# A state space layer beside projections: the scan over 512 steps becomes block Toeplitz products and a scan over 64 chunks

## The chip, the cores and the metric

The kernel runs on one core of a Trainium2 chip, in one launch. The metric is the device time of one execution in microseconds (us). The engines named below are TensorE (PE; its weight loads are PEld), VectorE (DVE), ScalarE (ACT), GpSimd (POOL) and SyncE (SP), which here issues nearly all DMAs. Each engine works through its own instructions in order.

## The reference

Three transformer-like blocks on 512 tokens of width 1024, in float32. The change lies in the first block, in its mixer: an attention and a state space branch are computed from the same projection and merged by gates. The state space branch has 16 groups of 16 channels with 64 complex states each:

```python
# per group g and state n: ab = exp((a_re + i a_im) * dt),  bb = (ab - 1) / (a_re + i a_im) * b
bu_re = einsum('bsgc,gnc->bsgn', ug, bb_re);  bu_im = einsum('bsgc,gnc->bsgn', ug, bb_im)
# x[t] = ab * x[t-1] + bu[t], complex, over the 512 tokens
_, _, xr, xi = lax.associative_scan(combine, (a_re_t, a_im_t, bu_re, bu_im), axis=1)
y = einsum('bsgn,gcn->bsgc', xr, c_re) - einsum('bsgn,gcn->bsgc', xi, c_im) + d_skip * ug
y = gelu(y);  return y * sigmoid(y @ w_glu + b_glu)
```

## The kernel before

**Layout.** Tokens lie along the free dimension (512), channels on the 128 partitions. A large product is made of three fp32r matmuls, high part times high part, times low part, and low times high (`mm3`, L105): so each weight tile is loaded, cast to its high part on ScalarE (L304) and given its low part on VectorE or GpSimd (L305). The class `Weights` keeps a fixed list of keys: three raw tiles, four split ones, loads up to three tiles ahead, issued by SP in the order of the list. A projection of one 128-channel tile is 24 matmuls of 512 columns.

**Order.** The order of instructions on every engine is written out by hand: it is the order in which the Python code issues them.

**The opening (`first_half`).** The input is normalised and modulated tile by tile into `xn`; for each of 8 tiles TensorE runs four matmuls for the attention's values (`banks`, L1126) and two for the state input (`us`, L1128), in plain float32. Beside it VectorE reduces the modulation's weights (`wa`), ScalarE modulates (L1078) and casts (L1082), and GpSimd builds, by doubling, the tables of cosines and sines (`Rotations.level`), and scales `b` (`scaled`). The callables of `more` say what is issued in which of the 8 steps.

**The stretch the change rewrites (`ssm_states`).** Eleven projections (`queue`, queries, keys and three gates) are interleaved with the scan. The states are taken two groups at a time, 2 x 64 on the partitions, in 8 rounds. In round i `drive` computes `bu` (six matmuls of 32 rows, copies by ScalarE), `table` doubles the rotation table to 512 steps (ScalarE, GpSimd, VectorE), `turn_back` and `turn_back2` rotate the drive back by the states' angle, `scan` runs two real scans of 512 steps with the decay `mag` (VectorE), `turn_forth` and `turned` rotate forth again, `emit` multiplies with `c` (four passes of float32), and `collect` adds the skip term into `y`, 32 rows at a time. The rotations' products are shared out between VectorE and GpSimd. The rounds are pipelined by one: round n+1 turns back while round n turns forth.

**After it.** `attention` runs 8 heads (scores `z`, softmax on VectorE and ScalarE, transposes, values) interleaved with more gate projections; its first projection still carries round 7's `emit` and `collect`. `gelu` and `glu` use `y` later. Then come the merging products, the first feed-forward part and the two further blocks, which the change does not touch.

Of the kernel before, what the change touches and what calls it, by code (L numbers as in the profile page):

```python
# [13 lines left out]
P = 128  # L14
# [8 lines left out]
_COLS = (("ident", P), ("ones", P), ("mask", P), ("count", 32), ("bada", 48), ("gmix", 8),  # L23
         ("gffn", 8), ("gfin", 8), ("bgate", 16), ("are", 8), ("aim", 8), ("ldt", 8), ("dskip", 2),
# [8 lines left out]
class Core:  # L33
# [4 lines left out]
    def __init__(self, ctx, tc, a):  # L38
# [17 lines left out]
        self.pav = ps("pav", 1)  # L56

# [4 lines left out]
        self.ident, self.ones = self.vec["ident"], self.vec["ones"]  # L62
        eps = self.const.tile([P, 1], F32, name="eps")
# [629 lines left out]

class SsmParams:


    def __init__(self, k, vec):
        self.k = k
        self.t = {n: k.const.tile([P, 8], F32, name=f"s_{n}") for n in (
            "dt", "mag", "ang", "n", "r", "sin", "cos", "half", "nr", "ni", "den", "fr", "fi", "x")}  # L700
        self.lr, self.li, self.ldt = vec["are"], vec["aim"], vec["ldt"]

    def load(self):
        self.b = self.k.tmp("b")
        self.k.nc.sync.dma_start(out=self.b, in_=self.k.a["bssm"])

    def decay(self):
        nc, t = self.k.nc, self.t
        nc.scalar.activation(t["dt"], self.ldt, AF.Exp)
        nc.gpsimd.tensor_tensor(t["mag"], self.lr, t["dt"], ALU.mult)  # L710
        nc.scalar.activation(t["mag"], t["mag"], AF.Exp)

    def angle(self):
# [8 lines left out]
        V.tensor_tensor(ang, self.li, t["dt"], ALU.mult)  # L722
# [41 lines left out]
    def scaled(self):  # L764
        k, t = self.k, self.t
        G = k.nc.gpsimd
        cut = lambda p, h: p[:, h * 256:h * 256 + 256].rearrange("p (i c) -> p i c", i=8)
        bre, bim = cut(self.b, 0), cut(self.b, 1)
        frb = t["fr"][:, :].unsqueeze(2).to_broadcast([P, 8, 32])
        fib = t["fi"][:, :].unsqueeze(2).to_broadcast([P, 8, 32])  # L770
        self.bb = k.tmp("bb")
        tt = k.tmp("bt")
        bbr, bbi, t1, t2 = cut(self.bb, 0), cut(self.bb, 1), cut(tt, 0), cut(tt, 1)
        G.tensor_tensor(bbr, bre, frb, ALU.mult)
        G.tensor_tensor(t1, bim, fib, ALU.mult)
        G.tensor_tensor(bbr, bbr, t1, ALU.subtract)
        G.tensor_tensor(bbi, bim, frb, ALU.mult)
        G.tensor_tensor(t2, bre, fib, ALU.mult)
        G.tensor_tensor(bbi, bbi, t2, ALU.add)

    def transpose(self):
        k = self.k
        ps = k.pz.tile([P, S], F32, tag="z", name=k.uid("bt"))
        for j in range(4):
            cs = slice(j * P, (j + 1) * P)
            k.nc.tensor.transpose(ps[:, cs], self.bb[:, cs], k.ident)
        self.bh, self.bl = k.gt("bth"), k.gt("btl")
        k.split(self.bh, self.bl, ps)


class Rotations:
# [3 lines left out]
    def __init__(self, k, params):  # L795
        self.k = k
        self.c = k.gt("c64", F32)[:, :].rearrange("p (i t) -> p i t", i=8)
        self.s = k.gt("s64", F32)[:, :].rearrange("p (i t) -> p i t", i=8)
        self.p = params.t["cos"], params.t["sin"]
        k.nc.vector.memset(self.c[:, :, 0:1], 1.0)  # L800
        k.nc.vector.memset(self.s[:, :, 0:1], 0.0)
        self.big = []

    def level(self, j):
        k, G = self.k, self.k.nc.gpsimd
        c, s = self.c, self.s
        pc, pn = self.p
        n = 1 << j
        if j < 6:
            lo, up = slice(0, n), slice(n, 2 * n)  # L810
            cb = pc[:, :].unsqueeze(2).to_broadcast([P, 8, n])
            sb = pn[:, :].unsqueeze(2).to_broadcast([P, 8, n])
            x = k.tmp("cx")[:, :].rearrange("p (i t) -> p i t", i=8)
            u, v = x[:, :, 0:n], x[:, :, 32:32 + n]
            G.tensor_tensor(u, c[:, :, lo], cb, ALU.mult)
            G.tensor_tensor(v, s[:, :, lo], sb, ALU.mult)
            G.tensor_tensor(c[:, :, up], u, v, ALU.subtract)
            G.tensor_tensor(u, c[:, :, lo], sb, ALU.mult)
            G.tensor_tensor(v, s[:, :, lo], cb, ALU.mult)
            G.tensor_tensor(s[:, :, up], u, v, ALU.add)  # L820
        else:
            self.big.append((pc, pn))
        if j < 8:
            c2 = k.const.tile([P, 8], F32, name=f"s_pc{j}")
            s2 = k.const.tile([P, 8], F32, name=f"s_ps{j}")
            x2 = k.const.tile([P, 8], F32, name=f"s_px{j}")
            G.tensor_tensor(x2, pn, pn, ALU.mult)
            G.tensor_tensor(c2, pc, pc, ALU.mult)
            G.tensor_tensor(s2, pc, pn, ALU.mult)
            G.tensor_tensor(c2, c2, x2, ALU.subtract)  # L830
            G.tensor_scalar(s2, s2, 2.0, 0.0, ALU.mult, ALU.add)
            self.p = c2, s2


class Ssm:

    def __init__(self, k, vec, params, tables):
        self.k, self.vec, self.params, self.tables = k, vec, params, tables  # L840
        self.u, self.uh, self.ul = [], [], []
        self.y = [k.gt("y", F32) for _ in range(2)]
        self.turn, self.half, self.work, self.bu, self.cw, self.ps = {}, {}, {}, {}, {}, {}
        for half in range(2):
            for ri in range(2):
                w = k.gt("cw", F32)[:, :].rearrange("p (q c) -> p q c", q=4)
                k.nc.sync.dma_start(out=w, in_=k.a["cssm"][half, ri])
                self.cw[half, ri] = w

    def table(self, i, j):  # L850

        if i > 7:
            return
        k, nc = self.k, self.k.nc
        c64, s64, big = self.tables.c, self.tables.s, self.tables.big
        if j == 0:
            c, s = k.tmp("rc"), k.tmp("rs")
            x, y = k.tmp("rx"), k.tmp("ry")
            nc.scalar.copy(c[:, :64], c64[:, i])
            nc.scalar.copy(s[:, :64], s64[:, i])  # L860
            self.turn[i] = c, s
            self.half[i] = x, y
        c, s = self.turn[i]
        x, y = self.half[i]
        n = 64 << j
        cj, sj = (p[:, i:i + 1] for p in big[j])
        lo, up, hi = slice(0, n), slice(n, 2 * n), slice(256, 256 + n)
        nc.scalar.activation(x[:, hi], s[:, lo], AF.Copy, scale=sj)
        nc.scalar.activation(y[:, hi], c[:, lo], AF.Copy, scale=sj)
        if j < 2:  # L870
            nc.scalar.activation(x[:, lo], c[:, lo], AF.Copy, scale=cj)
            nc.scalar.activation(y[:, lo], s[:, lo], AF.Copy, scale=cj)
# [1138 lines left out]
```

## Time and profile before

| | us |
|---|---|
| Median of 3 runs | 2599.25 (2597.18 to 2599.49) |
| The profiled execution | 2599.66 |
| Its span, first to last instruction | 2597.9 |
| TensorE busy | 2513.9 |
| VectorE busy | 1338.1 |
| ScalarE busy | 1021.3 |
| GpSimd busy | 659.3 |

Busy times are from the profile of one execution; its own time is 1.76 us longer than its span. The mean granted clock of TensorE was 0.986 of full speed. Of 40 equal slices of the span (65 us each), TensorE is busy nine tenths or more in all but the first three and the last; the first, with the opening, has 8 tenths, the next two, with the state space stretch, 7 each. The weights make most of the 252 MB that DMAs move, 97 GB/s in the mean.

### The profile page before, as it was taken

Reading aid. Unit: us, or ns where it says so; the run is one execution under the profiler, and the core shown is the slowest. Engines: PE = TensorE matmul, PEld = TensorE weight load, DVE = VectorE, ACT = ScalarE, POOL = GpSimd, SP = SyncE. Lnnn points to the kernel's source line nnn. Section 1 sums busy time; section 2 is a strip of 40 time slices with the busy share of each in tenths; the row PEclk is TensorE's granted clock in tenths of the full one; section 3 lists DMA queues with packets and bytes.
Section 4 is the critical chain, followed back from the end, with each engine's and each line's share of the span. In section 5 each row is a group of like instructions: output and inputs, shape, how many; then the busy total and the mean of one; then the engine's idle time right before and its main releaser. Section 6 shows DMA issues by size and latency. Waiting matters only on the chain.

```text
span 2597.9 us, 30110 instructions
## 1 busy us (share of the span) xinstructions
PE 2513.9 (97%) x11724; PEld 2060.5 (79%) x11724; DVE 1338.1 (52%) x1909; ACT 1021.3 (39%) x1667; POOL 659.3 (25%) x589
## 2 busy tenths in 40 slices
PE   8779999999999999999999999999999999999998
PEld 4557788888888888777888888888888778888887
DVE  6997675543534322885644432634423775633322
ACT  3536535332433322555533322433323655433322
POOL 7773121000311100564411100311102463311101
PEclk9889999999999999999999999999999999999999
DMA  6113453433223232212232333232232212222332
GB/s 261 49 58 113 148 173 122 138 98 98 83 97 97 96 98 92 74 49 82 82 98 98 95 91 99 82 98 97 85 106 79 73 52 95 77 97 96 93 97 69
DMA packets 80498, 252.14 MB, mean 97 GB/s; under 512 B 8930, under 2 KB 12770, under 8 KB 80356
## 3 DMA queue, kind: packets, MB, share of 16 engines
q1 hardware_dynamic: 79780, 249.70, 29.9%
q8 instruction: 92, 1.51, 0.2%
q10 hardware_dynamic: 576, 0.52, 0.1%
q14 instruction: 50, 0.41, 0.0%
HBM read 248.09 MB, written 2.10 MB: 96 GB/s over the span
## 4 chain that ended last, share of the span: by engine, by line
PE 80%; DVE 13%; ACT 3%; POOL 2%; issue 2%; DMA 0%; SPq 0%; DVEq 0%; ACTq 0%; POOLq 0%
PE mm L107 24%; PE mm L109 24%; PE mm L108 24%; PE mm L340 1%; DVE keep L1618 1%; DVE wa L503 1%; PE mm L1126 1%; PE n L368 1%; DVE wl L305 1%; PE z L1597 1%; POOL x L1522 1%; DVE fs L1514 1%; DVE acc L437 1%; DVE x L1522 1%; PE mm L608 1%
## 5 line engine op out<-in xcount | busy, mean ns | idle before, releaser
L305 DVE TENSOR_TENSOR wl<-wr,wh 128x1024 fp32r<-128x1024 f32 (+2 forms) x383 | 455.0, 1193 | 919.4 <-ACT wh L304 919.2
L304 ACT CAST wh<-wr 128x1024 fp32r<-128x1024 f32 (+3 forms) x444 | 430.8, 979 | 547.1 <-PE mm L108 507.9
L107 PE MATMUL mm<-xh,wh 128*128 128x512 f32 x1568 | 617.5, 394 | 0.1
L109 PE MATMUL mm<-xh,wl 128*128 128x512 f32 x1568 | 611.9, 390 | 0.0
L108 PE MATMUL mm<-xl,wh 128*128 128x512 f32 x1568 | 611.7, 390 | 0.0
L109 PEld LDWEIGHTS mm<-xh,wl 128*128 128x128 f32 x1568 | 295.3, 188 | 63.6 <-DVE wl L305 0.9
L107 PEld LDWEIGHTS mm<-xh,wh 128*128 128x128 f32 x1568 | 295.9, 189 | 61.2 <-issue 1.1
L107 PE MATMUL mm<-gh,wh 128*128 128x512 f32 (+1 forms) x936 | 343.8, 367 | 0.0
L108 PEld LDWEIGHTS mm<-xl,wh 128*128 128x128 f32 x1568 | 295.9, 189 | 59.8
L109 PE MATMUL mm<-gh,wl 128*128 128x512 f32 (+1 forms) x936 | 342.0, 365 | 0.0
L108 PE MATMUL mm<-gl,wh 128*128 128x512 f32 (+1 forms) x936 | 342.0, 365 | 0.0
L1566 POOL TENSOR_TENSOR ff<-ff,R 128x512 f32<-128x512 f32 x88 | 113.6, 1291 | 789.8 <-ACT ff L1565 789.8
L437 POOL TENSOR_TENSOR acc<-acc,sq 128x512 f32<-128x512 f32 (+1 forms) x85 | 93.9, 1104 | 716.0 <-ACT sq L424 715.2
L108 PEld LDWEIGHTS mm<-gl,wh 128*128 128x128 f32 x936 | 176.5, 189 | 28.8
L109 PEld LDWEIGHTS mm<-gh,wl 128*128 128x128 f32 x936 | 176.5, 189 | 28.5
L107 PEld LDWEIGHTS mm<-gh,wh 128*128 128x128 f32 x936 | 176.5, 189 | 28.5
L107 PE MATMUL mm<-uh,wh 128*128 128x512 f32 x424 | 174.4, 411 | 2.8 <-DVE vl L99 2.8
L305 POOL TENSOR_TENSOR wl<-wr,wh 128x1024 fp32r<-128x1024 f32 (+3 forms) x61 | 132.6, 2180 | 171.9 <-ACT wh L304 169.7
L109 PE MATMUL mm<-uh,wl 128*128 128x512 f32 x424 | 166.7, 393 | 0.3 <-DVE wl L305 0.3
L108 PE MATMUL mm<-ul,wh 128*128 128x512 f32 x424 | 166.5, 393 | 0.0
L98 ACT CAST gh<-ff 128x512 fp32r<-128x512 f32 x88 | 54.6, 621 | 171.0 <-DVE ff L1568 171.0
L1565 ACT ACTIVATE ff<-ff 128x512 f32<-128x512 f32 x88 | 55.6, 632 | 155.8 <-DVE ff L1564 155.8
(342 smaller groups left out, 3490.7 us busy)
## 6 DMA issues: line engine op xcount, KB each, us to landing
wr<-wg SPq DMA_DIRECT2D x88, 512.0 KB, 3.5
wr<-wu SPq DMA_DIRECT2D x88, 512.0 KB, 3.5
wr<-wd SPq DMA_DIRECT2D x80, 512.0 KB, 3.5
wr<-wi SPq DMA_DIRECT2D x56, 512.0 KB, 3.5
wa<-wada SPq DMA_DIRECT2D x64, 256.0 KB, 4.5
wr<-wup SPq DMA_DIRECT2D x32, 512.0 KB, 3.5
wr<-wo SPq DMA_DIRECT2D x24, 512.0 KB, 3.5
wr<-wd SPq DMA_DIRECT2D x32, 384.0 KB, 3.1
```

The source lines that it names most:

```text
L98: self.nc.scalar.copy(hi, raw)
L107: mm(out, wh, xh, start=start, stop=False, **kw)
L108: mm(out, wh, xl, start=False, stop=False, **kw)
L109: mm(out, wl, xh, start=False, stop=stop, **kw)
L304: self.k.nc.scalar.copy(hi[:, a:b], raw[:, a:b])
L305: e.tensor_tensor(lo[:, a:b], raw[:, a:b], hi[:, a:b].bitcast(F32), ALU.subtract)
L340: mm = lambda ps, w, x, a, b: k.nc.tensor.matmul(ps[:, cs], w, x, start=a, stop=b, skip_group_check=True)
L368: self.k.nc.tensor.matmul(self.cols[:, j:j + 1], src[:, j * P:(j + 1) * P], self.k.ones[:, 0:1], start=start and j == 0, stop=stop, skip_g ...
L437: engine.tensor_tensor(self.acc[:, c0:c1], self.acc[:, c0:c1], sq[:, c0:c1], ALU.add)
L1522: engine.tensor_tensor(x, x, self.f[i][:, cs], ALU.add)
L1565: nc.scalar.activation(t, t, AF.Silu)
L1566: nc.gpsimd.tensor_tensor(t, t, st.R, ALU.mult)
```

## The change

The 512 steps are cut into 64 chunks of L = 8 tokens. Inside a chunk the response of the channels to each other is a 128 x 128 matrix per group (16 channels by 8 tokens), block Toeplitz; from chunk to chunk the states go on by the eighth power of their decay.

- *Parameters.* The 16 groups now lie along the free dimension and real and imaginary parts fill the 128 partitions. `powers` (GpSimd) makes the powers 0 to 8 of `ab`; `Rotations` is rewritten: `square` (five small operations), `begin` (three squarings, then a table of 16 chunks, doubled four times), `finish` (ScalarE copies, two more doublings for two halves, the decay `mag8` spread over the table). `par.load` loads `c` beside `b`; `cssm` is no longer loaded in four pieces. `decay` gains an exponential for `mag8`.
- *Matrices.* `inward` (`H`) and `outward` (`N`) multiply `b` and `c` by the powers (three VectorE passes of 512 for each of four quarters, `_by_power`); `turn` transposes `H` into `G`; `response` multiplies `b` with `N` into the impulse response `K`, stores it to DRAM beside a padding of zeros, and `toeplitz` reads it back with overlapping rows, four DMAs of 128 runs of 512 bytes for each quarter; `order` reorders that on ScalarE into `T`.
- *Data.* `take` copies the state input, tokens of a chunk reversed, and stores it to DRAM; `fetch` reads it back with channels and tokens of the chunk on the partitions (`U`), 1024 runs of 256 bytes.
- *Stretch.* `drive` gives the states' input of a chunk (8 matmuls of 64 columns for each of two halves); `back` swaps real and imaginary parts by one matmul with a permuted identity (`exchange`, `ring`), rotates by three VectorE passes and scans 64 chunks of 8 groups in one scan of 512; `forth` rotates forth (again one `exchange`, three passes); `emit` adds T times U and N times x (16 matmuls of 64 columns for each half), copies, stores to DRAM by 1024 runs and reads back; `collect` adds the skip term, twice. All these matmuls are plain float32. The eleven projections each have lists `early`, `mid` (between weight tiles 4 and 5) and `end`.

`attention` loses its `emit(7)` and `collect(7)`.

```diff
...
+class Rotations:
...
+    def begin(self):
...
+        self.c16, self.s16, self.x = cut(w, 0, 16), cut(w, 1, 16), x
+        k.nc.gpsimd.memset(self.c16[:, :, 0:1], 1.0)
+        k.nc.gpsimd.memset(self.s16[:, :, 0:1], 0.0)
         for j in range(4):
+            n = 1 << j
+            lo, up = slice(0, n), slice(n, 2 * n)
+            self._double(self.c16[:, :, lo], self.s16[:, :, lo], self.c16[:, :, up], self.s16[:, :, up],
+                         slice(0, 16), n)
+            self.square()
...
+    def finish(self):
+        k = self.k
+        new = lambda n: k.gt(n, F32)[:, :].rearrange("p (g t) -> p g t", g=8)
+        gs = [slice(8 * h, 8 * h + 8) for h in range(2)]
+        self.c, self.s = [new("rc") for _ in gs], [new("rs") for _ in gs]
+        for h, g in enumerate(gs):
+            k.nc.scalar.copy(self.c[h][:, :, 0:16], self.c16[:, g])
+            k.nc.scalar.copy(self.s[h][:, :, 0:16], self.s16[:, g])
+            self._double(self.c16[:, g], self.s16[:, g], self.c[h][:, :, 16:32], self.s[h][:, :, 16:32], g, 16)
+        self.square()
+        for h, g in enumerate(gs):
+            c, s = self.c[h], self.s[h]
+            self._double(c[:, :, 0:32], s[:, :, 0:32], c[:, :, 32:64], s[:, :, 32:64], g, 32)
+        self.m = [new("rm") for _ in gs]
+        for m, g in zip(self.m, gs):
+            k.nc.scalar.copy(m, self.params.t["mag8"][:, g].unsqueeze(2).to_broadcast([P, 8, NCH]))
+            k.nc.gpsimd.memset(m[:, :, 0:1], 0.0)
...
 class Ssm:
...
+    def _by_power(self, q, x, y, m0):
         k, V = self.k, self.k.nc.vector
+        gs = slice(4 * q, 4 * q + 4)
+        full = [P, 4, 16, L]
+        cut = lambda t: t[:, :].rearrange("p (g c m) -> p g c m", g=4, c=16)
+        a, b = k.gt("hn", F32), k.tmp("hb")
+        for t, x, p in ((a, x, self.p.pr), (b, y, self.p.pi)):
+            V.tensor_tensor(cut(t), x[:, gs].unsqueeze(3).to_broadcast(full),
+                            p[:, gs, m0:m0 + L].unsqueeze(2).to_broadcast(full), ALU.mult)
+        V.tensor_tensor(a, a, b, ALU.add)
+        return a
...
+    def response(self, q):
+        k = self.k
+        ps = self.bank(k.pav)
+        for g in range(4):
+            k.nc.tensor.matmul(ps[0:16, g * P:(g + 1) * P], self.p.bx[:, 4 * q + g],
+                               self.N[q][:, g * P:(g + 1) * P], start=g == 0, stop=True,
+                               skip_group_check=True)
+        t = k.tmp("K")
+        k.nc.scalar.copy(t[0:16].rearrange("p (g m c) -> p g m c", g=4, c=16),
+                         ps[0:16].rearrange("p (g c m) -> p g m c", g=4, c=16))
+        k.nc.sync.dma_start(out=self.kd[:, 4 * q:4 * q + 4, 112:],
+                            in_=t[0:16].rearrange("p (g n) -> p g n", g=4))
...
+    def toeplitz(self, q):
+        k = self.k
+        t = k.tmp("T")
+        for g in range(4):
+            a = self.kd[:, 4 * q + g, 0:P]
+            a = bass.AP(tensor=a.tensor, offset=a.offset, ap=[[16 * 240, 16], [16, L], [1, P]])
+            k.nc.sync.dma_start(out=t[:, g * P:(g + 1) * P], in_=a)
+        self.raw.append(t)
...
+    def order(self, q):
+        k = self.k
+        t = k.gt("T", F32)
+        k.nc.scalar.copy(t[:, :].rearrange("p (g c j) -> p g c j", g=4, c=16),
+                         self.raw[q][:, :].rearrange("p (g j c) -> p g c j", g=4, c=16))
+        self.T.append(t)
...
+    def take(self, m, ps):
+        k = self.k
+        u = k.gt("us", F32)[:, :].rearrange("p (j t) -> p j t", j=L)
+        k.nc.scalar.copy(u, ps[:, :].rearrange("p (t j) -> p j t", j=L)[:, ::-1])
+        d = k.dram.tile([P, L, NCH], F32, name=f"du{m}")
+        k.nc.sync.dma_start(out=d, in_=u)
+        self.u.append(u)
+        self.d = getattr(self, "d", []) + [d]
...
+    def fetch(self, m):
+        k = self.k
+        U = k.gt("U", F32)[:, :].rearrange("p (g t) -> p g t", g=8)
+        src = self.d[m][:].rearrange("(g c) m t -> g (c m) t", g=8).rearrange("g q t -> q g t")
+        k.nc.sync.dma_start(out=U, in_=src)
+        self.U.append(U)
...
+    def back(self, h):
+        k, V = self.k, self.k.nc.vector
+        v = self.vs.pop(h)
+        ps = self.exchange(v)
+        b = k.tmp("wb")
+        c, s, m = (t[h][:, :].rearrange("p g t -> p (g t)") for t in (self.rot.c, self.rot.s, self.rot.m))
+        V.tensor_tensor(v, v, c, ALU.mult)
+        V.tensor_tensor(b, ps, s, ALU.mult)
+        V.tensor_tensor(v, v, b, ALU.subtract)
+        z = self.z[h] = k.gt("z", F32)
+        V.tensor_tensor_scan(z, m, v, 0.0, ALU.mult, ALU.add)
...
+    def emit(self, h):
+        k = self.k
+        ps = self.bank()
+        mm = k.nc.tensor.matmul
+        for g in range(8):
+            q, i = divmod(8 * h + g, 4)
+            cs, gs = slice(g * NCH, (g + 1) * NCH), slice(i * P, (i + 1) * P)
+            mm(ps[:, cs], self.T[q][:, gs], self.U[h][:, g], start=g == 0, stop=False, skip_group_check=True)
+            mm(ps[:, cs], self.N[q][:, gs], self.x[h][:, g], start=False, stop=True, skip_group_check=True)
+        t = k.tmp("yt")[:, :].rearrange("p (g t) -> p g t", g=8)
+        k.nc.scalar.copy(t, ps[:, :].rearrange("p (g t) -> p g t", g=8))
+        d = self.yd = k.dram.tile([8, P, NCH], F32, name=f"dy{h}")
+        k.nc.sync.dma_start(out=d[:].rearrange("g q t -> q g t"), in_=t)
+        y = self.yp[h] = k.tmp("yp")[:, :].rearrange("p (j t) -> p j t", j=L)
+        k.nc.sync.dma_start(out=y, in_=d[:].rearrange("g (c j) t -> (g c) j t", j=L))
...
@@ first_half @@
+    par.powers()
+    par.factor()
+    ssm = Ssm(k, vec, par, rot)
+    more = {0: par.scaled, 2: rot.begin, 4: rot.finish, 6: lambda: [ssm.inward(q) for q in range(2)],
+            7: lambda: [ssm.inward(q) for q in range(2, 4)]}
     for i in range(KT):
...
+    for m in range(2):
+        ssm.take(m, ub[m])
     split_value(0)
     k.w.prepare()
+    for m in range(2):
+        ssm.fetch(m)
+    late = [lambda tt=tt: split_value(tt) for tt in range(1, 4)]
...
@@ ssm_states @@
+    each = lambda f, *qs: [lambda q=q: f(q) for q in qs]
+    early = {0: late[0:1], 1: late[1:2], 2: late[2:3]}
+    mid = {0: each(ssm.turn, 0), 1: each(ssm.turn, 2), 2: each(ssm.response, 0), 3: each(ssm.response, 1),
+           4: each(ssm.response, 2) + each(ssm.back, 0), 6: each(ssm.forth, 0), 7: each(ssm.order, 0, 1, 2, 3),
+           8: each(ssm.emit, 0)}
+    end = {0: each(ssm.turn, 1) + each(ssm.outward, 0), 1: each(ssm.turn, 3) + each(ssm.outward, 1, 2),
+           2: each(ssm.outward, 3) + each(ssm.drive, 0), 3: each(ssm.drive, 1) + each(ssm.response, 3),
+           4: each(ssm.back, 1), 5: each(ssm.toeplitz, 0, 1, 2, 3), 6: each(ssm.forth, 1),
+           8: each(ssm.emit, 1), 10: each(ssm.collect, 0, 1)}
+    for n in range(11):
         if n == 7:
             dist = k.gt("dist", F32), k.gt("lnc", F32)
             for j, t in enumerate(dist):
                 k.nc.sync.dma_start(out=t, in_=k.a["dist"][:, j])
         queue.begin(False)
+        for f in early.get(n, ()):
+            f()
+        k.w.prepare()
         queue.run(0, 4)
+        for f in mid.get(n, ()):
+            f()
         queue.run(4, KT)
         queue.end()
+        for f in end.get(n, ()):
+            f()
```

## Rows read from the trace of the kernel before

**Rows 1.** the page's engine totals: busy us, share of the span, instructions.

```profile
PE 2513.9 (97%) x11724; PEld 2060.5 (79%) x11724; DVE 1338.1 (52%) x1909; ACT 1021.3 (39%) x1667; POOL 659.3 (25%) x589
```

**Rows 2.** busy us by stretch: length, engines (instructions), granted clock, DMA share, GB/s.

```profile
22.35:66.30 43.95, 43.95 (x100) 19.55 (x101) 30.12 (x56) 14.50 (x27) 34.80 (x61) 1.00 0.59 219
66.30:195.70 129.40, 100.07 (x343) 67.08 (x341) 123.22 (x120) 54.97 (x133) 92.83 (x68) 0.88 0.16 53
84.50:90.20 5.70, 5.70 (x26) 4.44 (x25) 5.70 (x6) 2.16 (x4) 2.74 (x3) 1.00 0.30 95
```

**Rows 3.** timeline of TensorE: start us, us, line, tiles, count [idle before, releaser].

```profile
60.82 3.60 PE L1126 MATMUL mm<-wr,xn 128*128 128x512 f32 x8
...
65.97 0.60 PE L786 MATMUL bt<-cst,bb 128*128 128x128 f32 x4
66.32 0.48 PE L107 MATMUL mm<-uh,wh 128*128 128x512 f32 x1
...
78.58 0.80 PE L107 MATMUL mm<-uh,wh 128*128 128x512 f32 x1 [2.75 <-DVE vl L99]
...
81.71 0.40 PE L108 MATMUL mm<-ul,wh 128*128 128x512 f32 x1
...
195.72 0.49 PE L107 MATMUL z<-qh,qh 64*128 64x512 f32 x1
```

**Rows 4.** VectorE's groups, 66.3 to 195.7: line, tiles, count | busy us, mean ns | idle.

```profile
L305 DVE TENSOR_TENSOR wl<-wr,wh 128x1024 fp32r<-128x1024 f32 x12 | 18.9, 1580 | 0.3 <-ACT wh L304 0.3
...
L916 DVE TENSOR_TENSOR p<-bu,rc 128x512 f32<-128x512 f32 x8 | 14.1, 1767 | 0.0
...
L926 DVE TENSOR_TENSOR_SCAN bu<-s_mag,p 128x512 f32<-128x512 f32 x8 | 9.8, 1226 | 0.3
...
L915 DVE TENSOR_TENSOR p<-bu,rc 128x512 f32<-128x512 f32 x8 | 5.5, 683 | 2.4 <-ACT bu L893 2.4
```

**Rows 5.** TensorE's waits, 66 to 198: who, for whom, us in total, times, longest.

```profile
PE em L950 <- DVE y L957: 19.5, 4, 7.6
```

**Rows 6.** ScalarE's groups, 66.3 to 195.7, columns as in rows 4.

```profile
L304 ACT CAST wh<-wr 128x1024 fp32r<-128x1024 f32 x13 | 13.5, 1043 | 0.0
L893 ACT COPY bu<-dr 128x512 f32<-128x512 f32 x16 | 8.5, 580 | 0.0
```

**Rows 7.** timelines of ScalarE and VectorE, end of the input loop.

```profile
49.98 0.81 ACT L1078 ACTIVATE xn<-xn,shift,gain 128x512 f32<-128x512 f32 x1 [2.47 <-DVE shift L1075]
...
62.49 0.69 DVE L99 TENSOR_TENSOR vl<-mm,vh 128x512 fp32r<-128x512 f32 x1 [7.43 <-ACT vh L98]
```

**Rows 8.** timeline of TensorE, a one-column float32 matmul near the end.

```profile
2576.71 0.95 PE L368 MATMUL n<-cst,acc 128*128 128x1 f32 x8
```

**Rows 9.** GpSimd: busy us of 25 to 50, and its timeline.

```profile
25.00:50.00 25.00, 24.05 (x40) 1.00 0.66 251
...
51.50 0.20 POOL L831 TENSOR_SCALAR s_ps<-s_ps 128x8 f32<-128x8 f32 x1
51.66 0.62 POOL L774 TENSOR_TENSOR bb<-b,s_fr 128x256 f32<-128x256 f32 x1
...
56.19 0.72 POOL L779 TENSOR_TENSOR bb<-bb,bt 128x256 f32<-128x256 f32 x1
...
63.42 0.46 POOL L873 TENSOR_TENSOR rc<-rx 128x128 f32<-128x128 f32 x1 [5.95 <-ACT rx L871]
```

**Rows 10.** timeline of SP's queue.

```profile
20.68 0.33 SPq L705 DMA_DIRECT2D b<-bssm  x1
```

**Rows 11.** DMA issues: tiles, queue, count, KB each, median us to landing.

```profile
wr<-wi SPq DMA_DIRECT2D x56, 512.0 KB, 3.5
...
wa<-wada SPq DMA_DIRECT2D x64, 256.0 KB, 4.5
...
wur<-wi SPq DMA_DIRECT2D x4, 256.0 KB, 8.1
...
wr<-pw SPq DMA_DIRECT2D x4, 64.0 KB, 2.5
```

More of the change, by code (lines that the diff above doesn't have):

```diff
@@ L776, in scaled @@
[L776 to L788, printed above, removed]
+        cut = lambda p, h: p[:, h * 256:h * 256 + 256].rearrange("p (g c) -> p g c", g=16)
@@ new lines, in _double @@
+    def _double(self, c, s, c2, s2, gs, n):
+        G = self.k.nc.gpsimd
+        ng = gs.stop - gs.start
+        pc, pn = self.p
+        cb = pc[:, gs].unsqueeze(2).to_broadcast([P, ng, n])
+        sb = pn[:, gs].unsqueeze(2).to_broadcast([P, ng, n])
+        u, v = (self.x[:, h * 256:h * 256 + ng * n].rearrange("p (g t) -> p g t", g=ng) for h in range(2))
+        G.tensor_tensor(u, c, cb, ALU.mult)
+        G.tensor_tensor(v, s, sb, ALU.mult)
+        G.tensor_tensor(c2, u, v, ALU.subtract)
+        G.tensor_tensor(u, c, sb, ALU.mult)
+        G.tensor_tensor(v, s, cb, ALU.mult)
+        G.tensor_tensor(s2, u, v, ALU.add)
@@ L835 @@
 class Ssm:
     def __init__(self, k, vec, params, tables):
[L840 to L848, printed above, removed]
@@ L953, in collect @@
[L953 to L959 removed]
+        self.k, self.vec, self.p, self.rot = k, vec, params, tables
+        self.u, self.U = [], []
+        self.H, self.N, self.G, self.T, self.raw = [], [], [], [], []
@@ new lines, in toeplitz @@
+    def toeplitz(self, q):
+        k = self.k
+        t = k.tmp("T")
+        for g in range(4):
+            a = self.kd[:, 4 * q + g, 0:P]
[8 more added lines that the diff above has]
+        self.T.append(t)
@@ new lines, in drive, with exchange @@
+    def drive(self, h):
+        k = self.k
+        ps = self.bank()
+        for g in range(8):
+            q, i = divmod(8 * h + g, 4)
+            k.nc.tensor.matmul(ps[:, g * NCH:(g + 1) * NCH], self.G[q][:, i * P:(i + 1) * P], self.U[h][:, g],
+                               start=g == 0, stop=True, skip_group_check=True)
+        v = self.vs[h] = k.gt("vs", F32)
+        k.nc.scalar.copy(v, ps)
+    def exchange(self, t):
+        ps = self.bank()
+        self.k.nc.tensor.matmul(ps, self.k.ring, t, start=True, stop=True)
+        return ps
@@ new lines, in emit @@
+    def emit(self, h):
+        k = self.k
+        ps = self.bank()
+        mm = k.nc.tensor.matmul
+        for g in range(8):
+            q, i = divmod(8 * h + g, 4)
+            cs, gs = slice(g * NCH, (g + 1) * NCH), slice(i * P, (i + 1) * P)
[7 more added lines that the diff above has]
+        k.nc.sync.dma_start(out=y, in_=d[:].rearrange("g (c j) t -> (g c) j t", j=L))
@@ L1045, in first_half @@
     rot = Rotations(k, par)
-    rot.level(0)
     mod.act()
@@ L1202, in ssm_states @@
 def ssm_states(k, ssm, queue, late):
-    w = k.w
-    queue.begin(False)
-    queue.run(0, 4)
-    ssm.drive(0)
-    queue.run(4, KT)
-    ssm.turn_back(0)
-    ssm.turn_back2(0)
-    ssm.table(1, 2)
-    late[0]()
-    ssm.drive(1)
-    ssm.scan(0)
-    w.prepare()
-    queue.end()
-    for n in range(8):
+    each = lambda f, *qs: [lambda q=q: f(q) for q in qs]
[8 more added lines that the diff above has]
+    for n in range(11):
         if n == 7:
@@ L1273, in attention @@
             prev.values()
-        else:
-            ssm.emit(7)
         queue.run(6, KT)
-        if not prev:
-            ssm.collect(7)
         queue.end()
@@ L1954, in layout @@
         v[n] = _cols(f[src])
-    v["ldt"] = _cols(np.repeat(f["log_dt"][0], 64))
+    two = lambda re, im: np.concatenate([re, im], axis=0)
+    v["are"], v["aim"] = (two(f[n][0].T, f[n][0].T) for n in ("a_re", "a_im"))
+    v["ldt"] = np.repeat(f["log_dt"][0][None], P, axis=0)
     o["cst"] = np.ascontiguousarray(np.concatenate([v[n] for n, _ in _COLS], axis=1))
```

317 lines of the change are left out of this document (116 added, 201 removed).

## The prediction

> **What bounds the kernel now.** The busy totals come first: TensorE is busy 2513.9 us, 97% of the span, so most of the time can't shrink by moving other engines' work [rows 1]. Then the stretches [rows 2]. While TensorE computes the values and the state input (22.35 to 66.30) it is busy all the time. From 66.30 to 195.70, where eleven projections run beside the state space scan, it is busy 100 of 129 us at a granted clock of 0.88, while VectorE is busy 123.2. That is the only stretch the change touches deeply, and VectorE sets it. One undisturbed projection fills 84.50 to 90.20, 5.7 us [rows 2], so eleven are 62.7: some 67 us of the 129.4 are the scan's price. The groups of VectorE's lines show how it comes about [rows 4]: the weights' low parts are 18.9 us, and nearly all the rest are the scan's passes over 512 time steps, several at 1.1 to 1.8 us where L915, the same operation, takes 0.68. The waits agree: TensorE's largest is 19.5 us at `em`, behind VectorE [rows 5]. Attention's first scores start at 195.72 [rows 3]. The profiled execution took 2599.66 us, 1.76 of it around its span; the median of the runs is 0.4 lower.
>
> **The change, part by part.** The sum is over the distance from 66.32 (first projection) to 195.72 (first scores) [rows 3], 129.4 us now; the number of projections stays.
>
> *VectorE.* Gone are eight groups of rotations and collects and sixteen scans of 512 steps. What stays or comes, at undisturbed durations [rows 4]: 11 weight parts (1.58 in the mean), 11 low parts of queries, keys and values, 12 passes of `outward`, 6 of `back`, 6 of `forth` and 2 of `collect` at about 0.68, and 2 scans at 1.23: 17.4 + 25.2 + 2.5 = 45 us. ScalarE has 11 weight casts at 1.04, 14 casts or copies of results and 16 new copies, these thirty at 0.58 [rows 6]: 29 us. Both fit beside TensorE's time below, so TensorE becomes the bound of the stretch.
>
> *TensorE.* The new work is plain float32, two passes a matmul. Eight passes of 512 columns take 3.60 us [rows 3], so a matmul 0.90 and the four of `exchange` 3.6. Four transposes take 65.97 to 66.32 = 0.35 [rows 3], the four `turn` 1.4. For 64 and 128 columns there is no row. From below they cost what one column costs, 8 passes in 0.95 us, 0.24 for two [rows 8]; from above that and the columns at the 512-column rate, 0.35 and 0.46. Weight loads hide partly under columns, so I stay near the lower row: 0.27 and 0.30. `drive` and `emit` have 16 + 32 of the first (13.0), `response` 16 of the second (4.8). Sum 22.8, between 20 and 29. The old `dr` and `em` matmuls go with the 129.4.
>
> *The start of the stretch: what is late next.* Now the last step of the input loop starts at 60.82 [rows 3], with `xn` ready ten microseconds earlier (ScalarE's last L1078 starts at 49.98) [rows 7]. The change puts `rot.finish` into step 4, and its first ScalarE copies read `c16` and `s16`, which GpSimd makes in `rot.begin`. ScalarE works in order: its casts and the modulation of step 7, queued behind these copies, wait for GpSimd. When is `c16` done? `scaled` needs `b`, issued at 20.68 [rows 10]; loads of that size took 8.1 us then [rows 11], so it starts at 28.8. Its six operations took 51.66 to 56.91 = 5.2 us before [rows 9], so 34.0. `rot.begin` has 56 operations up to `c16`. GpSimd did 40 in 24.05 us between 25 and 50, 0.60 each beside a busy VectorE [rows 9]; 26 of the 56 fit until VectorE's reductions are over, just before 49.98, and the other 30 run alone at 0.16 (start to start, 51.50 to 51.66) to 0.46 (128 elements a partition) [rows 9], some 7.5 us. So `c16` at 57, between 52 and 66. Then ScalarE has four short copies of about 0.3, two of 0.58, a cast and the modulation (0.81) [rows 6, 7]: `xn` at 60.6, just in time, and TensorE ends the loop at 66.3 as now.
>
> But VectorE waits for the same cast before the low part of step 6, and the four `inward` now stand ahead of the value split that frees the first result bank: 59.8 + 0.7, six passes, a weight part 1.5, 0.7, six passes, 0.7. A pass costs 0.68 alone and 1.77 beside GpSimd (L915 and L916 [rows 4]); GpSimd's 31 operations of `finish` last until about 72, so I take 1.2 for the first six and 0.9 for the others: 76.0. The first projection starts 9.7 us late. The least is 2.4: the two copies of the state input now go ahead of the value split on ScalarE. The most is 29: `c16` at 66, all passes at 1.77. After idling TensorE starts at the lower of its two levels: after 2.75 us of idle, seven matmuls took 78.58 to 81.71 = 3.1 us [rows 3] instead of 1.6, so 1.5 more. ScalarE's longer opening (one more exponential) adds 0.3.
>
> *Queues.* SP issues every load of weights, in order, and now also the relayouts: two stores and two `fetch`, four stores of `K`, sixteen loads of `toeplitz`, a store and a load for each `emit`, each load waiting until the store before it has landed. Weights are loaded three projections ahead, 512 KB in 3.5 us [rows 11], and a projection with its share of the new work now takes 7.8 us, so some 20 us of SP waiting are covered. `drive` reads `fetch` some 20 us after its issue, `order` the toeplitz loads 11 us after, `collect` the last load 17 us after the first store. Issues cost SP 0.33 each [rows 10], the sixteen 5.3, and a 64 KB load lands 2.5 us later [rows 11]: just covered. I allow 2 us of waits in the stretch, between 0 and 8. The four loads of `cssm` (1 MB) go and 256 KB comes into the opening; both lie beside TensorE.
>
> Sum: 9.7 + 1.5 + 62.7 + 22.8 + 2.0 = 98.7 against 129.4, so 30.7 less; the last two `em` matmuls inside attention go (1.8), the opening costs 0.3: 32.2. 2599.66 - 32.2 = 2567.5, and 0.4 off for the median: **2567 us**.
>
> *A rule against the change.* Both `fetch` and both stores of `emit` move 1024 runs of 256 bytes. The nearest row here, 128 runs of 512 bytes, lands in 2.5 us [rows 11]; none has so many short runs. The Trainium skill, "DMA: Bandwidth & Descriptors", sections Specifications and Why small descriptors are slow, says that a transfer under 512 bytes becomes a read-modify-write, and that a 256-byte descriptor on HBM loses about 27%. By the page's 27% the 256 KB load of 4.5 us would become an estimated 5.7 us, and the sum would stay as it is; rival 3 asks for far more.
>
> **The rivals.**
> 1. *The front is hidden.* GpSimd has `c16` by 52 and the `inward` passes run at 0.68. For it: VectorE idles 7.4 us there now [rows 7]. The gap is 2.4 instead of 9.7: 2560; with the small matmuls and the waits at their lower ends too, 2555.
> 2. *GpSimd is late.* With its 62 operations from `scaled` on at 0.8 us, `c16` is ready at 78, the first projection starts some 19 us behind it, at 97 instead of 76: 2588. For it: 0.60 is a mean over operations mostly smaller than the new ones [rows 9]. Against it: VectorE has little to do from 50 on.
> 3. *The relayouts bind, and it is slower.* If time goes by runs, the eightfold runs of a 256 KB load (4.5 us [rows 11], 128 runs) give up to X = 36 us for each. `fetch` is issued behind a weight load at about 79, so the second lands at 79 + 2X, while its `drive` is due at 105; the stores and the load of `emit` have 2X + 4.5 against 17.5 us. The losses are 2X - 26 and 2X - 13; together they eat the 32.2 at X = 18. At X = 24 they are 57, and the time is 2624. For it: SP and its queue are shared with the weights. Against it: 64 KB and 256 KB differ by 2 us only.
> 4. *It doesn't do what it says*, and the stretch stays VectorE's: 45 us of work can't fill it; doubled by contention it would be 90, as long as TensorE's part. That would be 2570 to 2580.
>
> **How the numbers follow.** The forecast 0.50 (own range 2558 to 2577), rival 1 0.17, rival 2 with SP's longer waits, up to 2594, 0.20, rival 3 0.08, rival 4 0.05. All lower ends of the terms give 2555, all upper ends 2599. The range that leaves out 2 in 10: 2552 to 2592. A measurement of this kernel can tell some 0.2%, 5 us, from no change. Faster by more: the forecast, rivals 1 and 4 and most of rival 2, 0.88; within: 0.05, from the edges of rivals 2 and 3; slower: 0.07, rival 3 above X = 19 and a GpSimd later than rival 2 has it.
>
> **What would show it.** First scores at about 164 instead of 195.7, and from 80 on a granted clock of 1.00 with TensorE busy. From 66 to 76 TensorE idle, ended by the value split on VectorE; ScalarE waiting for GpSimd at the copies of `c16` until about 57. `drive` and `emit` at 0.27 a matmul, `response` at 0.30. VectorE's passes at about 0.7 from 80 on. After attention's start nothing moves by more than 2 us. I am wrong if TensorE waits at `drive`, at `emit` or behind `collect` for more than 8 us in all, if weights come late, or if the small matmuls take over 0.45 us.

## The result, and the profile after

The changed kernel takes **2560.59 us** (median of 4 runs, 2559.24 to 2561.6), the one before 2598.88 on the same chip (4 runs): a ratio of 0.9853, 95% interval 0.9836 to 0.987, 38.3 us faster. The forecast was 2567, range 2552 to 2592. The profiled execution took 2561.6 us, span 2559.8.

The page's engine totals, as in rows 1:

```profile
PE 2496.7 (98%) x11792; PEld 2059.9 (80%) x11792; DVE 1261.8 (49%) x1848; ACT 998.2 (39%) x1576; POOL 582.4 (23%) x556
```

Busy time by stretch, columns as in rows 2: the input loop, the idle gap behind it, and the eleven projections up to attention's first scores.

```profile
22.35:66.70 44.35, 44.05 (x96) 19.01 (x96) 32.44 (x60) 14.56 (x25) 36.00 (x80) 1.00 0.50 188
66.70:73.47 6.77, 0.05 (x2) 0.01 (x1) 6.70 (x10) 3.55 (x5) 6.66 (x9) 0.89 0.66 195
73.47:157.07 83.60, 83.60 (x416) 67.63 (x416) 41.62 (x52) 27.23 (x38) 8.53 (x14) 0.97 0.39 117
```

Where VectorE was busy 123 of 129 us and TensorE 100 [rows 2], TensorE is now busy in all 83.6 us and VectorE in half of them. TensorE's `em` waits [rows 5] are gone; one new wait of 6.7 us stands ahead of the first projection. TensorE's timeline, as in rows 3:

```profile
61.32 3.70 PE L1227 MATMUL mm<-wr,xn 128*128 128x512 f32 x8
64.86 1.88 PE L1229 MATMUL us<-xn,wur 128*128 128x512 f32 x4
73.47 0.79 PE L111 MATMUL mm<-uh,wh 128*128 128x512 f32 x1 [6.72 <-DVE vl L103]
...
91.66 1.05 PE L950 MATMUL sp<-hn,bb 128*16 128x128 f32 x8
92.64 0.50 PE L111 MATMUL mm<-uh,wh 128*128 128x512 f32 x1
...
95.49 1.89 PE L1000 MATMUL sp<-U,G 128*128 128x64 f32 x16
97.19 0.48 PE L111 MATMUL mm<-uh,wh 128*128 128x512 f32 x1
...
136.15 0.33 PE L1045 MATMUL sp<-U,T 128*128 128x64 f32 x2
...
139.63 0.48 PE L111 MATMUL mm<-uh,wh 128*128 128x512 f32 x1
...
157.07 0.49 PE L111 MATMUL z<-qh,qh 64*128 64x512 f32 x1
```

The first scores moved from 195.72 [rows 3] to 157.07, 38.65 us; from there to the end nothing is won (2402.2 us before, 2402.7 now). From start to next start, `drive` (8 matmuls) takes 1.70 us, `emit` (16) 3.48 and `response` (4) 0.98: 0.21, 0.22 and 0.245 a matmul. ScalarE and VectorE at the end of the input loop, as in rows 7:

```profile
56.92 0.30 ACT L878 COPY rc<-r 128x128 f32<-128x128 f32 x1 [10.08 <-POOL r L867]
...
59.94 0.61 ACT L1181 CAST uh<-xn 128x512 fp32r<-128x512 f32 x1
...
67.26 0.59 ACT L102 CAST vh<-mm 128x512 fp32r<-128x512 f32 x1
```

```profile
60.59 0.84 DVE L1185 TENSOR_TENSOR ul<-xn,uh 128x512 fp32r<-128x512 f32 x1 [9.94 <-ACT uh L1181]
61.35 0.89 DVE L921 TENSOR_TENSOR hn<-bb,pw 128x512 f32<-128x512 f32 x1
...
71.82 0.99 DVE L923 TENSOR_TENSOR hn<-hn,hb 128x512 f32<-128x512 f32 x1
72.73 0.68 DVE L103 TENSOR_TENSOR vl<-mm,vh 128x512 fp32r<-128x512 f32 x1
```

ScalarE waits 10 us for GpSimd's `c16`, VectorE waits for the cast queued behind that copy, and its twelve `inward` passes (the first at 61.35, the last at 71.82) keep the value split till 72.73. Its high part, ScalarE's cast `vh`, was done at 67.85, so 4.9 of the 6.7 us of idle are VectorE's queue; the other 1.8 are ScalarE's copies and that cast (1.1) and the low part itself (0.7).

### The profile page after: what moved, and what is told of

Same layout as the page of the kernel before. It is cut to its first block, busy times and chain, and to the rows that moved or that the text cites. A ratio compares the mean times of both kernels' runs of the same rounds, so it can differ in the third digit from the quotient of the medians.

```text
span 2559.8 us, 30104 instructions
## 1 busy us (share of the span) xinstructions
PE 2496.7 (98%) x11792; PEld 2059.9 (80%) x11792; DVE 1261.8 (49%) x1848; ACT 998.2 (39%) x1576; POOL 582.4 (23%) x556
## 2 busy tenths in 40 slices
DMA packets 87697, 254.80 MB, mean 100 GB/s; under 512 B 13698, under 2 KB 19842, under 8 KB 87556
## 4 chain that ended last, share of the span: by engine, by line
PE 82%; DVE 10%; ACT 3%; POOL 2%; issue 1%; DMA 1%; SPq 0%; DVEq 0%; ACTq 0%; POOLq 0%
PE mm L111 25%; PE mm L113 25%; PE mm L112 25%; PE mm L344 2%; DVE keep L1683 1%; DVE wa L507 1%; PE z L1662 1%; POOL x L1587 1%; DVE fs L1579 1%; DVE x L1587 1%; DMA wa<-wada 1%; DVE acc L441 1%; PE z L1661 1%; DVE xl L107 1%; PE mm L612 1%
## 5 line engine op out<-in xcount | busy, mean ns | idle before, releaser
L309 DVE TENSOR_TENSOR wl<-wr,wh 128x1024 fp32r<-128x1024 f32 (+2 forms) x383 | 449.8, 1179 | 935.9 <-ACT wh L308 935.7
L112 PEld LDWEIGHTS mm<-gl,wh 128*128 128x128 f32 x936 | 176.5, 189 | 28.6
L309 POOL TENSOR_TENSOR wl<-wr,wh 128x1024 fp32r<-128x1024 f32 (+2 forms) x61 | 132.7, 2181 | 245.8 <-ACT wh L308 243.7
```

The costliest lines, as they stand in the source:

```text
L112: mm(out, wh, xl, start=False, stop=False, **kw)
L309: e.tensor_tensor(lo[:, a:b], raw[:, a:b], hi[:, a:b].bitcast(F32), ALU.subtract)
```

## The experiments

**1. The passes behind the value split.** All four groups of `inward` go out of the loop; the split goes first, ahead of the two copies of `take` too. In part:

```
-    more = {0: par.scaled, 2: rot.begin, 4: rot.finish, 6: lambda: [ssm.inward(q) for q in range(2)],
-            7: lambda: [ssm.inward(q) for q in range(2, 4)]}
+    more = {0: par.scaled, 2: rot.begin, 4: rot.finish, }
...
+    split_value(0)
+    ssm.inward(0)
     for m in range(2):
         ssm.take(m, ub[m])
-    split_value(0)
     k.w.prepare()
+    ssm.inward(1)
...
+    early = {0: late[0:1] + each(ssm.inward, 2), 1: late[1:2] + each(ssm.inward, 3), 2: late[2:3]}
...
+           2: each(ssm.turn, 3) + each(ssm.response, 0),
```

> The changed kernel takes 2560.6 us; its first projection starts at 73.47, 6.7 us after the loop over the input ends. Here the twelve passes of `inward` go behind the first value split: one group before the first projection, one beside it, two in the next two projections; `turn` of the last two groups moves half a projection later. Theory A (the idle 6.7 us are VectorE's passes standing ahead of the value split): first projection at 68.3 (66.7, a ScalarE cast of 0.6 and a low part of 0.7), less of the stretch at the lower clock, 2555 us (2553.5 to 2556.5). Rival B (the passes are only moved: TensorE now waits for them at the first two `turn`, two waits of 2 to 3 us): first projection early, scores where they were, 2559 to 2561.

Measured: 2552.8 us (5 runs), 7.8 less than the changed kernel. TensorE's timeline, ScalarE's cast of the first result, and TensorE's waits (who, for whom, us in total, times, longest):

```profile
64.86 1.88 PE L1228 MATMUL us<-xn,wur 128*128 128x512 f32 x4
66.18 0.79 PE L111 MATMUL mm<-uh,wh 128*128 128x512 f32 x1
66.81 0.40 PE L112 MATMUL mm<-ul,wh 128*128 128x512 f32 x1
...
73.19 0.63 PE L940 MATMUL sp<-cst,hn 128*128 128x128 f32 x4 [0.52 <-DVE hn L923]
...
84.11 0.63 PE L940 MATMUL sp<-cst,hn 128*128 128x128 f32 x4 [1.49 <-DVE hn L923]
```

```profile
62.49 0.58 ACT L102 CAST vh<-mm 128x512 fp32r<-128x512 f32 x1 [0.42 <-PE mm L1226]
```

```profile
PE sp L940 <- DVE hn L923: 2.0, 2, 1.5
```

Theory A holds, and more came than it asked for. The last step of the loop does its value matmuls ahead of the state input's, so the first result bank is complete before the loop ends; ScalarE's cast of it starts at 62.49, beside the last matmuls, and no gap is left at all, so no matmul runs at the lower clock either. B is right about two waits, but they cost only 2.0. The edit takes away both VectorE's queue and ScalarE's copies ahead of the split; this run doesn't tell the two apart, and their shares (4.9 and 1.1) are read from the trace of the changed kernel.

**2. The wait for `c16` taken away alone.**

```
-    more = {0: par.scaled, 2: rot.begin, 4: rot.finish, 6: lambda: [ssm.inward(q) for q in range(2)],
+    more = {0: par.scaled, 2: rot.begin, 6: lambda: [ssm.inward(0), ssm.inward(1), rot.finish()],
```

> The changed kernel, with `rot.finish` moved from step 4 of the input loop to step 6, behind the first two `inward`, so that no cast or modulation on ScalarE is queued behind the copies that wait for GpSimd's `c16`. Theory A (the wait for `c16` is what makes `inward` late): ScalarE's last cast at some 51 instead of 59.94, VectorE begins `inward` at some 52.5, at 1.0 to 1.2 us a pass beside GpSimd has done all twelve by 67, first projection at 68.5 to 69.5, 2556 us (2554.5 to 2557.5); GpSimd's `finish` lasts till about 90, which `back` at 100 doesn't feel. Rival C (VectorE and GpSimd slow each other wherever they meet): passes at 1.77 from 52.5 on last till 74 and GpSimd's `c16` comes at 62, first projection at 75, 2561 to 2563.

Measured: 2557.94 us (4 runs), 2.7 less, a little more time than A allowed. VectorE, then TensorE:

```profile
56.21 0.69 DVE L923 TENSOR_TENSOR hn<-hn,hb 128x512 f32<-128x512 f32 x1
63.71 1.30 DVE L309 TENSOR_TENSOR wl<-wr,wh 128x1024 fp32r<-128x1024 f32 x1 [6.81 <-ACT wh L308]
```

```profile
71.50 0.80 PE L111 MATMUL mm<-uh,wh 128*128 128x512 f32 x1 [4.59 <-DVE vl L103]
```

The passes of two groups were done at 56.9, as A said. But the weights' cast of step 6 stands behind `rot.finish` on ScalarE, which I had overlooked: VectorE waits 6.8 us for it, with the other two groups queued behind. The wait moved by one instruction; 2 of the 6.7 us gap went. C's slow passes didn't come: 0.69 to 0.84 each for the first six. The other half of C did in part: ScalarE's copy of `c16` starts at 59.62 instead of 56.92.

**3. Both edits.** The diff of 1, with `more` as follows:

```
-    more = {0: par.scaled, 2: rot.begin, 4: rot.finish, 6: lambda: [ssm.inward(q) for q in range(2)],
-            7: lambda: [ssm.inward(q) for q in range(2, 4)]}
+    more = {0: par.scaled, 2: rot.begin, 6: rot.finish}
```

> Both edits: `rot.finish` behind the input loop's step 6 and the `inward` passes behind the first value split. Theory A: one cause, removed twice, so hardly more than the first edit alone: the loop ends 0.4 us earlier, since step 7 no longer waits for the cast: 2554.5 us (2553 to 2556). If the two edits each took away a part of their own (rival: two separate delays of 5 us each), 2550. This is the version that I expect to be the fastest.

Measured: 2553.69 us (4 runs, 2551.92 to 2555.03), not to be told from the first edit alone; in its trace the first scores start at 150.0, in that one's at 150.1. The two edits remove one delay. I had expected this to be the fastest version; experiment 8 is faster.

**4. Three times the relayouts.**

```
-        k.nc.sync.dma_start(out=U, in_=src)
+        for _ in range(3):
+            k.nc.sync.dma_start(out=U, in_=src)
```

and the same at the store and the load of `emit`.

> The changed kernel with three of its relayout transfers issued three times each, one behind the other: both `fetch`, both stores of `emit` and both loads behind them (12 more transfers of 1024 runs of 256 bytes). Theory H (the relayouts are hidden with room to spare): `fetch` lands 16 us ahead of its `drive` and feels nothing; the last `collect` has 7.6 us from its store's issue, of which store and load take 5.2, so if the copies overlap in the queue the time stays at 2560.6 (2559 to 2563), and if each waits for the one before it the loss is at most 8: 2568. Rival 3 of the forecast (they are close to binding, time goes by runs): the fetches come late too and the weight loads behind them with it, over 2575.

Measured: 2574.56 us (4 runs), 14.0 more. SP's queue with two of its waits, then VectorE and TensorE:

```profile
73.91 14.30 SPq L992 DMA_DIRECT2D U<-du  x6
...
139.61 6.07 SPq L1052 DMA_DIRECT2D dy<-yt  x3
147.88 5.68 SPq L1055 DMA_DIRECT2D yp<-dy  x3
153.66 6.30 SPq L1052 DMA_DIRECT2D dy<-yt  x3
162.17 5.65 SPq L1055 DMA_DIRECT2D yp<-dy  x3
```

```profile
SPq L1052 <- DMA dy<-yt: 9.9, 4, 2.9
SPq L1055 <- DMA yp<-dy: 9.2, 4, 2.4
```

```profile
156.10 1.26 DVE L1060 SCALAR_TENSOR_TENSOR y<-us,cst,yp 128x512 f32<-128x512 f32 x1 [2.48 <-DMA yp<-dy]
170.22 1.14 DVE L1060 SCALAR_TENSOR_TENSOR y<-us,cst,yp 128x512 f32<-128x512 f32 x1 [12.86 <-DMA yp<-dy]
```

```profile
172.78 0.79 PE L111 MATMUL z<-qh,qh 64*128 64x512 f32 x1 [8.82 <-DVE st L661]
173.37 0.62 PE L112 MATMUL z<-ql,qh 64*128 64x512 f32 x1
```

The expectation is wrong about the loads: only eight of the twelve copies have 1024 runs of 256 bytes, for the loads `yp` take, for each partition, one run of 2 KB. The trace agrees: 22082 packets under 512 bytes against 13698 in the changed kernel, 8384 more, about the 8192 of the eight copies of `fetch` and of the stores. Both theories failed in part. The `fetch` loads, tripled, still cost nothing: the scores start at 156.2. All of the loss comes at the second `collect`: each copy waited for the one before it, and I had counted only the second group's transfers, though its store stands in SP's queue behind the first group's loads. VectorE waits 12.9 us, the first head's softmax is queued behind it, TensorE idles 8.8 us and comes back at its lower level (0.62 a matmul, granted clock 0.81 between 156 and 200). With one copy the second load lands at some 152.0 (issued at 149.4, 2.6 to land) for a `collect` at 154.5 and scores at 157: a reserve of a few microseconds, in the one place of the change where a relayout is close to the end of the chain.

**5. The small matmuls twice.** In `drive` likewise (only the new lines are shown, without `skip_group_check`):

```
+            for twice in range(2):
+                mm(ps[:, cs], self.T[q][:, gs], self.U[h][:, g], start=g + twice == 0, stop=False)
+                mm(ps[:, cs], self.N[q][:, gs], self.x[h][:, g], start=False, stop=twice == 1)
```

> The changed kernel with every matmul of `drive` and `emit` issued twice (48 more of 64 columns; the outputs of `emit` are twice as large, so the result differs). Theory T (TensorE alone bounds the stretch from 73 to 157): the time grows by the whole price of the 48, at the 0.22 us of the profile 10.5 us: 2571 us. With the forecast's 0.27: 13.0, 2573.6. Rival (another engine or the relayouts still set part of the stretch): less than 5 us, below 2566.

Measured: 2571.75 us (4 runs), 11.2 more; from first projection to first scores 93.78 us instead of 83.60, 0.21 for each of the 48. Theory T holds: what TensorE gets, the time gets.

```profile
73.36 0.79 PE L111 MATMUL mm<-uh,wh 128*128 128x512 f32 x1 [6.72 <-DVE vl L103]
...
167.14 0.49 PE L111 MATMUL z<-qh,qh 64*128 64x512 f32 x1
```

**6. The kernel before without the turn behind its scans.**

```
-        G.tensor_tensor(p4, zr, s, ALU.mult)
-        V.tensor_tensor(p1, zr, c, ALU.mult)
-        V.scalar_tensor_tensor(p3, zi, -1.0, c, ALU.mult, ALU.mult)
-        G.tensor_tensor(zi, zi, s, ALU.mult)
+        self.work[i] = zr, zr, zi, p4, zi
...
-        G.tensor_tensor(p3, p3, p4, ALU.subtract)
-        V.tensor_tensor(p1, p1, zi, ALU.subtract)
```

> The kernel before, without the turn behind its scans: `turn_forth` and `turned` are left out and `emit` takes the scans' own outputs, so 24 VectorE passes (28.6 us in the stretch from 66 to 196) and 24 GpSimd passes (46.7 us) are gone, and TensorE's work is as it was; the result differs. Theory V (VectorE sets that stretch): the stretch shrinks by the 28.6, as far as TensorE's 100 us of busy time let it: 2571 us (2567 to 2577). Rival (it was TensorE at its lower clock or the chain through ScalarE's tables that set it, and VectorE only filled the time): less than 10 us, above 2589.

Measured: 2563.63 us (4 runs), 35.3 less than before. Its stretch up to the first scores, and two of VectorE's groups there (60 to 170), as in rows 2 and 4:

```profile
66.30:159.30 93.00, 89.86 (x340) 63.63 (x338) 88.32 (x99) 54.06 (x133) 46.91 (x44) 0.96 0.22 75
```

```profile
L305 DVE TENSOR_TENSOR wl<-wr,wh 128x1024 fp32r<-128x1024 f32 x13 | 16.8, 1296 | 0.3 <-ACT wh L304 0.3
...
L916 DVE TENSOR_TENSOR p<-bu,rc 128x512 f32<-128x512 f32 x8 | 7.6, 948 | 0.0
```

Theory V holds, though the time lies below its 2567: the 28.6 us of VectorE's work were worth more than their own time. With GpSimd's 24 passes gone, L916 fell from 1.77 to 0.95 us and a weight part from 1.58 to 1.30 [rows 4]; TensorE, waiting less, went from a granted clock of 0.88 to 0.96, and its busy time for the same matmuls from 100 to 90. The Trainium skill, "SBUF — State Buffer", section SBUF: two separate sides, says that VectorE, in operations with two inputs in SBUF, and a GpSimd operation that reads it hold a shared pair of ports in turn, whole instructions at a time; L916 with and without these passes is in line with that. Since GpSimd's 46.7 us went with VectorE's 28.6, the run doesn't show what either would have given alone; that VectorE set the stretch rests on its 123.2 busy us of 129.4 as well, against GpSimd's 92.8 [rows 2].

**7. VectorE's work put back into the changed kernel.** Four passes whose output nobody reads, ahead of each projection's matmuls.

```
+        t = k.tmp("ex")
+        for _ in range(4):
+            k.nc.vector.tensor_tensor(t, k.ring[:, 0:1].to_broadcast([P, S]),
+                                      k.ring[:, 0:1].to_broadcast([P, S]), ALU.mult)
         queue.run(0, 4)
```

> The changed kernel with four further VectorE passes of 128x512 in each of the eleven projections, whose output nobody reads: 44 passes at 0.6 to 0.7, 26 to 30 us, as much as the turn behind the old scans cost VectorE. Theory T (TensorE alone bounds the stretch, VectorE is busy 43 of 87 us): 2561 us (2559 to 2564). Rival (what VectorE has to do in time for TensorE is nearly late): each projection waits for its weights' low part or a result's, above 2568.

Measured: 2560.57 us (4 runs, 2557.87 to 2561.68): no difference. The passes, and the stretch:

```profile
L1311 DVE TENSOR_TENSOR ex<-cst 128x512 f32<-128x512 f32 x44 | 31.8, 722 | 1.1
```

```profile
73.40:157.00 83.60, 83.60 (x423) 67.79 (x423) 70.45 (x95) 28.45 (x40) 10.48 (x14) 0.98 0.38 116
```

The stretch is cut near the changed kernel's times; this run's own, from 72.93 to 155.57, is 82.6 us. VectorE at 70 of 84 us still costs nothing. The 31.8 us of added passes are free here, where GpSimd is busy only 10.5.

**8. The passes in the order in which they are due.** As experiment 1, with both first groups straight behind the split, the third alone beside the first projection, the fourth at its end, and `rot.finish` last. In part, against experiment 1:

```
     split_value(0)
     ssm.inward(0)
+    ssm.inward(1)
...
     for m in range(2):
         ssm.fetch(m)
+    rot.finish()
...
+    early = {0: late[0:1] + each(ssm.inward, 2), 1: late[1:2], 2: late[2:3]}
...
+    end = {0: each(ssm.turn, 1) + each(ssm.inward, 3) + each(ssm.outward, 0), 1: each(ssm.outward, 1, 2),
```

> As the earlier version with the `inward` passes behind the value split (2552.8 us), with each group's passes put where VectorE is idle ahead of its `turn`: two groups right behind the first low part of the values, the third before the second projection's weights, the fourth at the end of the first projection; and `rot.finish` behind the loop, where no cast waits for GpSimd. Theory: the two waits of TensorE at `turn` (0.5 and 1.5 us) go, 2551 us (2549.5 to 2552.5). Rival: GpSimd's `finish`, begun later, and VectorE's passes slow each other and the waits stay: 2553 to 2555.

Measured: **2551.21 us** (5 runs, 2550.12 to 2552.51), ratio to the kernel before 0.9816 (0.9802 to 0.9829): the lowest median, 9.4 below the changed kernel. Against experiment 1's 2552.8 the runs overlap; that the waits went is shown by the trace, where one is left in the stretch:

```profile
PE sp L950 <- DVE hn L923: 0.5, 1, 0.5
```

```profile
65.31:147.24 81.93, 81.45 (x419) 66.08 (x417) 51.44 (x61) 32.36 (x49) 16.41 (x25) 1.00 0.43 129
```

## Why the prediction was right

**The bound.** VectorE set the old stretch ([rows 2] and experiment 6) and TensorE sets the new one (5 and 7). That was the main step, and it held. Rival 4 is out.

**The start of the stretch.** Forecast: first projection at 76.0; measured: 73.47. `c16` at 57 was met: its copy starts at 56.92. But ScalarE's second copy waited another 1.1 us for `s16`, which the forecast had ready at the same time, so VectorE's low part began at 60.59 instead of 59.8. The passes were mis-sized the other way: from start to start 0.83 in the mean for the first six and 0.70 for the others instead of 1.2 and 0.9, 3.4 us less. Together that is the 2.5 us. It was GpSimd that was slowed more. The same operation of `square`, while VectorE waits and beside its passes:

```profile
58.40 0.21 POOL L836 TENSOR_TENSOR c<-c 128x16 f32<-128x16 f32 x1
...
68.64 0.66 POOL L836 TENSOR_TENSOR c<-c 128x16 f32<-128x16 f32 x1
```

`finish` lasted until 82.3 instead of 72. Rival 2's late GpSimd came only there, where nobody waited for it. Rival 1 (a gap of 2.4) is out in its mechanism, though its 2560 is the time that was measured: the gap was 7.2, and other terms were smaller.

**From first projection to first scores.** Forecast 89.0 (1.5 + 62.7 + 22.8 + 2.0), measured 83.6. The waits: none instead of 2.0. The lower clock: the first twelve matmuls take 5.28 us (73.47 to 78.75, where `turn` begins); in experiment 1, without a gap, they take 3.14 (66.18 to 69.32), so 2.1 instead of 1.5 (2.4, if the next twelve of the same trace, 2.84, are the measure). What is left for the small matmuls is 83.6 - 62.7 - 2.1 = 18.8 instead of 22.8. This is the largest error. Read directly, `drive` and `emit` took 10.5 instead of 13.0 and `response` 3.9 instead of 4.8, 3.4 of the 4.0; the rest is not assigned. I took 0.27 and 0.30, a little over the one-column matmul's 0.24 [rows 8]. That row runs from the first start to the last end; read the same way, the eight matmuls of `drive` take 1.89, 0.24 each too, while from start to start each adds only 0.21. So 64 columns cost no more than one column, which is the lower end of the forecast. Together -2.0 + 0.6 - 4.0 = -5.4.

**Behind the first scores.** I took 1.8 off for the last `em` pair inside attention. It didn't show; that part of the trace is 0.5 us longer. The 0.3 of a longer opening came (TensorE starts the loop at 22.64 instead of 22.35), but the measured 73.47 holds it already. So 2.5 + 5.4 + 0.3 on the one side and 1.8 + 0.5 on the other: 32.2 became 38.1 between the two spans. The mechanism was right, and the errors of size partly cancelled.

**The relayouts.** Rival 3 needed X = 18 us; measured, the two kinds of transfer with 1024 runs of 256 bytes landed in 4.8 (`fetch`, `U`) and 2.6 (the store `dy`). The issues, landing times in the last column:

```profile
T<-kd SPq DMA_DIRECT2D x16, 64.0 KB, 2.2
du<-us SPq DMA_DIRECT2D x2, 256.0 KB, 5.7
U<-du SPq DMA_DIRECT2D x2, 256.0 KB, 4.8
dy<-yt SPq DMA_DIRECT2D x2, 256.0 KB, 2.6
yp<-dy SPq DMA_DIRECT2D x2, 256.0 KB, 2.6
```

The other two 256 KB transfers of the list, `du` and `yp`, have 128 runs of 2 KB and took 5.7 and 2.6: `dy` and `yp`, issued one behind the other, are equal with eightfold and single runs, and `U` is near the 4.5 us of a 256 KB load in 128 runs [rows 11]. So eight times the runs cost hardly any time here. The loss of 27% that the Trainium skill, "DMA: Bandwidth & Descriptors", section Why small descriptors are slow, gives for 256 bytes doesn't show in `dy` against `yp`, a store against a load; no run moves the same data in the same direction in both patterns. The prediction's estimate of 5.7 put the 27% on top of 4.5; the Trainium skill, in the same section, counts it as 3 of 11 cycles, which would make an estimated 6.2. One step was lucky: SP spent 10.2 us on the sixteen `toeplitz` issues, not 5.3, and the last one made `order` wait; nobody was late for it.

```profile
120.71 10.21 SPq L966 DMA_DIRECT2D T<-kd  x16
...
132.49 1.09 ACT L973 COPY T<-T 128x512 f32<-128x512 f32 x1 [0.66 <-DMA T<-kd]
```

## What to carry to other kernels

When a stretch changes its bound, price the new bound's added instructions and then look at its two ends: here the inside was free of waits, and the 9 us that experiment 8 still won lay in what was queued ahead of its first instruction. A setup edit that makes one engine wait for another belongs behind the casts, splits and copies that the bound engine needs, on every queue it passes: moving it one step too little only changed which cast was late. Passes of VectorE and GpSimd that run beside each other can cost more than their own duration: taken out together in experiment 6, they gave back 35 us where VectorE's own were 28.6.

## What the runs showed of the hardware

- A plain float32 matmul of 64 columns and 128 weights takes 0.21 to 0.22 us in a row of its kind; eight take 1.89 from first start to last end, 0.24 each, as the one-column ones do [rows 8]. Doubled, 48 of them cost 10.2 us.
- Contention fell mostly on one side: at the opening of the stretch VectorE's passes took 0.7 to 1.0 us, where 0.68 is undisturbed, while GpSimd's small products took 0.66 instead of 0.21 and `finish` ended 10 us later than forecast. In the old stretch VectorE's L916 took 1.77. Which of the two engines pays was not settled.
- An idle TensorE costs twice: 6.7 us of idle brought the lower level for some 5 us more (granted clock 0.50 from 73.47 to 78.75), 2.1 to 2.4 of them lost. Without the gap, in experiments 1 and 8, no matmul ran at it, and the granted clock of the stretch was 1.00.
